# Eight weight tiles instead of six in the expert stages, and 2 KB runs for the context's weights

## The chip, the cores and the metric

One Trainium2 chip, one core. The metric is the device time of one execution in microseconds (us), the median of several runs. Tensors are float32 throughout. The core's engines are TensorE (PE; its weight loads are listed apart as PEld), VectorE (DVE), ScalarE (ACT), GpSimd (POOL) and SyncE (SP), and 16 DMA engines move data between device memory and the on-chip buffers. All weight loads here are issued by SP, in one queue and in the order of the program.

## What is computed

A network of two blocks over 256 tokens of 1024 features. The first block has two layers, each an attention or a retention followed by a mixture of 32 experts. The second block has two layers over the same tokens and over a separate context of 256 positions, each a mixer and a feed-forward of 2816 hidden units. The context needs its full first layer and part of its second, and does not depend on the tokens:

```python
# experts: each token goes to 2 of 32; every expert's weights are read
def expert_block(args):
    xb, e = args
    a, b = jnp.split(xb @ w_gu[e], 2, axis=-1)        # [1024, 2 * 512]
    return (jax.nn.silu(a) * b) @ w_down[e]           # [512, 1024]

# second block, for the tokens and for the context
def swiglu(h, w_gu, w_down):                          # [1024, 2 * 2816], [2816, 1024]
    gate, up = jnp.split(h @ w_gu, 2, axis=-1)
    return (jax.nn.silu(gate) * up) @ w_down

pc = (rmsnorm(xc, norm1_g[l]) * (1.0 + scc1) + shc1) @ w_in[l] + b_in[l]   # w_in [1024, 3088]
...
xc = xc + gc1 * (y_c @ w_out[l])
xc = xc + gc2 * swiglu(rmsnorm(xc, norm2_g[l]) * (1.0 + scc2) + shc2, w_gu[l], w_down[l])
```

## The kernel before

Features or tokens lie on 128 partitions. The program runs through stages: attention (from 0 us), the first expert stage (`moe(0)`), retention, the second expert stage (`moe(1)`), then the tokens' two layers of the second block. Beside each stage runs other work that does not depend on it: the context's mixer of layer 0 beside `moe(0)`, and the context's feed-forward of layer 0 and short mixer of layer 1 beside `moe(1)`. `weave` (L1737) traces the two together, R1 = 0.8 or R3 = 0.88 steps of the context's work for each step of the experts'. A scheduler then sets each engine's order from priorities; the engines run their lists in order.

Weights come as tiles of 1 MB ([128 partitions, 2048 numbers], 8 KB on each partition) from the pool `wp`, which has six of them (L97). `wt` (L126) hands them out. At the start of an expert stage three more places, `e0` to `e2` of another pool, are used once each. A load waits on SP until PE has read the tile that lay in its place before.

- `moe` (L848): the experts in eight groups of four, q = 0 to 7. A group loads 16 tiles for gate and up (L153, two experts' 128 rows of 1024 columns, runs of 4 KB) and 8 tiles for down. The products with gate and up are L956, with down L976. `gather` (L885) picks the next group's tokens. `combine` (L979) adds a group's result to the tokens: a copy `ys`, four products (L986) into PSUM banks `g`, four additions by DVE (L988).
- `fs` (L417): a product with features on partitions, for the context in plain float32 (mode "f"): blocks of 256 columns of all 1024 rows, one tile each, in runs of 1 KB. 16 products (L430; the trace lists each as two records) fill one bank `g`; then ACT or DVE reads it, and the step ends (`yield`).
- `ts` (L437): a product with tokens on partitions; blocks of 512 columns and 512 rows, runs of 2 KB.
- `ffn` (L1396): the feed-forward, in mode "f" in 11 rounds of 256 hidden units, three steps each: gate by `fs`, up by `fs`, and `down` (L1407) of the round before: four pairs of products (L1416), each into a bank `g` of its own, which `residual` (L369) multiplies (L372) and adds (L373) on DVE.
- `mixer` (L1263): the input products by `fs` and `ts`; the convolution's gate columns and its value columns are two calls of `fs` of 256 columns, which lie side by side in `w_in`.

There are four banks `g` (L100) for all of this, and two double banks `m` for the experts' sums.

Of the kernel before, what the change touches and what calls it, by code (L numbers as in the profile page):

```python
# [19 lines left out]
NEG = -1e30  # L20
RS = -8192.0                    # what rsqrt's scaled form carries
NE, CAP, FF = 32, 32, 512
R0, R1, R2, R3, R4 = 1.8, 0.8, 1.0, 0.88, 0.7           # steps of other work per step of the main path
AHEAD = 200                     # instructions that what the others wait for goes ahead of
TAPS = 6                        # convolution taps between other work
PIECE, WS = 512, 6              # elements per partition split at a time; pieces on chip
# [3 lines left out]
# columns of the constant array  # L30
C_ID, C_LE, C_LT, C_GE, C_ONE = 0, 128, 256, 384, 512
C_Z, C_LOW, C_UP = 640, 768, 896          # 0 where col <= row / col >= row, else NEG
C_IOTA, C_GRP, C_I8 = 1024, 1056, 1088
C_SEL, C_OFF = 1096, 1112                 # row 32 j + i, column i; rows of scales: what to add, 1 / RS
C_COS, C_SIN, C_RET = 1116, 1372, 1628         # rotary, decay
NCST = C_RET + 4 * 384

# modulation vectors: which third of the columns of w_mod, and which two of its quarters
# [4 lines left out]
def constants():  # L43
    """Tables that depend on shapes alone."""
# [35 lines left out]
class Tags:  # L80
    """A pool, some of whose tags lie in another one under other names."""
# [10 lines left out]
class Net:  # L92
    def __init__(self, tc, I, out, es):
# [8 lines left out]
        self.flip, self.extra = 0, []  # L102
        self.later, self.pending, self.taken = [], [], False
        self.early, self.hold = -99, None                  # pieces of weights whose low parts GpSimd makes

# [7 lines left out]
    def bank(self):  # L113
        """One bank, from the other pool while g's are taken."""
        return self.m()[:, 0:512] if self.taken else self.g()

    def two(self, mode, apart=False):
        """Two banks."""
        if mode == "f":
            return self.g(), self.g()  # L120
        if apart:
            return self.m()[:, 0:512], self.m()[:, 0:512]
        t = self.m()
        return t[:, 0:512], t[:, 512:1024]

    def wt(self, name):  # L126
        """A weight tile; some lie in the places of tiles that are no longer needed."""
        if self.extra:
            return self.pre.tile([P, 2048], F32, tag=self.extra.pop(0), name=name)
        return self.wp.tile([P, 2048], F32, tag="w", name=name)  # L130

    def wload(self, src):
        """One tile of weights: rows (k p) of src on the partitions."""
# [6 lines left out]
    def wtile(self):  # L140
        """A weight tile as [P, 2, D]."""
        return self.wt("w").rearrange("p (b d) -> p b d", b=2)

    def gain(self, src, g):
        """src [D] on all partitions."""
# [3 lines left out]
    def wload2(self, src):  # L149
        """The same rows of two experts: src [2, P, 1024]."""  # L150
# [16 lines left out]
    def affine(self, o, i, scale, bias=None, eng=None):  # L167
        """o = i * scale + bias, per partition."""
# [10 lines left out]
    def split(self, pool, tag, src, shape=None, low=None):  # L179
        """src = H + L exactly, both in the tensor engine's one-pass format."""  # L180
# [12 lines left out]
    def wparts(self, w, mode):  # L193
        """Parts of a weight tile [P, k, c]: each a function of (row block, first column, last column)."""
# [15 lines left out]
    def pairs(self, a, b):  # L210
        """Products that make up a.b for operands in parts."""
        return [(a[0], b[0])] if len(a) == 1 else [(a[0], b[0]), (a[1], b[0]), (a[0], b[1])]

    def rstd(self, ss, n, eps=EPS):
        """1/sqrt(ss/n + eps)"""
# [4 lines left out]
    def rsqrt(self, h, scaled=False):  # L220
        """1/sqrt(h): a first guess from the exponent's bits, then Newton's steps. Scaled: RS times it, for one column."""
# [9 lines left out]
        for _ in range(3):  # L231
            if scaled:                  # y = c / sqrt(h) to (y h y - 3 c c) y = -2 c^3 / sqrt(h)
# [13 lines left out]
    def rms(self, x, b, junk, act=False):  # L246
        """rstd of token block b of x [P, 2, D]"""
# [12 lines left out]
    def transposed(self, xn, b, cb):  # L260
        """cb(k, psum [P, n, 128]) for the feature chunks k .. k + n of token block b of xn [P, 2, D]"""
# [7 lines left out]
    def normed(self, pool, x, g, sh, mode, junk, tag="x", first=None, xn=None):  # L269
        """Parts of (rms-normalised x, times g plus sh)^T, each [P, 8, T]; sh and g / RS [P, D].  # L270
# [1567 lines left out]
```

## Time and profile before

| | |
|---|---|
| median of 3 runs | 2349.72 us (2346.77 to 2353.50) |
| span of the profiled execution, first to last instruction | 2346.0 us |
| PE busy | 2127.2 us, 91% of the span |
| DVE, ACT, POOL busy | 1060.9, 695.6, 172.9 us |
| moved by DMA | 686.64 MB, on average 293 GB/s |
| first expert stage, about | 208 to 762 us |
| second expert stage, about | 985 to 1635 us |

The profiled execution's own time is its span; what lies around the span in a timed run is not shown, and the median of the runs is 3.7 us above it. The page cuts the span into 40 slices of 58.65 us and gives for each the busy share of every engine, PE's granted clock and the mean busy share of the 16 DMA engines in tenths, and the GB/s moved. A table of stretches gives the same for any stretch, with idle time as length less busy time. A share of DMA of 1 or a little more in a stretch means that the DMA engines did not rest in it. A list of waits gives, for each line and tile, what it waited for: total, times, and the longest, in us.

### The profile page before, as it was taken

The numbers are of one execution on the slowest core, as the hardware profiler recorded it, in microseconds if no ns is written. First come the engines' busy times: TensorE is split into PE (matmuls) and PEld (weight loads), VectorE is DVE, ScalarE is ACT, GpSimd is POOL, SyncE is SP. The second block draws the span as 40 slices with busy tenths as digits, with TensorE's granted clock in tenths as the row PEclk, the third lists the DMA queues.
The fourth block names the chain that finished last, engine by engine and source line by source line (L and its number), as shares of the span: only waits on it lengthen the run. The fifth ranks groups of instructions, "written<-read, shape, count | busy, mean of one in ns | idle before, by whom it ended". The sixth has DMA issues, their size and how long they took to land. (4 is left out here: it accounts for less than half of the span.)

```text
span 2346.0 us, 32803 instructions
## 1 busy us (share of the span) xinstructions
PE 2127.2 (91%) x12844; PEld 1433.4 (61%) x12845; DVE 1060.9 (45%) x2513; ACT 695.6 (30%) x1420; POOL 172.9 (7%) x194
## 2 busy tenths in 40 slices
PE   8998899889877999989899999987998998998998
PEld 7765445344222776855444444334787997787997
DVE  6556053322101766531121221415778556777555
ACT  4353111211000434520000000012555554554554
POOL 1001000000000111010000000001212002102000
PEclk9999999999988999989999999999999999999999
DMA  8864999999999977579999999999756554555551
GB/s 257 313 245 166 350 399 392 369 399 378 379 409 384 323 281 246 203 268 382 391 398 393 399 390 390 367 356 346 256 162 202 188 190 156 187 181 171 192 185 63
DMA packets 305320, 686.64 MB, mean 293 GB/s; under 512 B 22056, under 2 KB 163784, under 8 KB 298888
## 3 DMA queue, kind: packets, MB, share of 16 engines
q1 hardware_dynamic: 305096, 684.45, 79.9%
q8 instruction: 103, 1.69, 0.3%
q14 instruction: 57, 0.47, 0.1%
q10 hardware_dynamic: 64, 0.03, 0.0%
HBM read 681.78 MB, written 2.62 MB: 292 GB/s over the span
## 5 line engine op out<-in xcount | busy, mean ns | idle before, releaser
L190 DVE TENSOR_TENSOR wl<-w,wh 128x512 fp32r<-128x512 f32 x574 | 396.3, 707 | 252.4 <-ACT wh L185 233.7
L185 ACT CAST wh<-w 128x512 fp32r<-128x512 f32 x600 | 364.3, 621 | 355.5 <-PE psm L430 111.6
L956 PE MATMUL psm<-w,xg 128*32 128x512 f32 x2048 | 319.8, 632 | 61.8 <-DMA w<-in_expert_w_gu_dram 55.0
L430 PE MATMUL psg<-xt,w 128*128 128x256 f32 x1056 | 235.8, 381 | 20.5 <-DMA w<-in_w_gu_dram 11.3
L430 PEld LDWEIGHTS psg<-xt,w 128*128 128x128 f32 x1056 | 198.0, 190 | 71.1 <-issue 38.6
L956 PEld LDWEIGHTS psm<-w,xg 128*32 128x32 f32 x2048 | 66.4, 112 | 270.6 <-issue 150.4
L430 PE MATMUL psg<-xh,wh 128*128 128x256 f32 x608 | 177.2, 291 | 3.9 <-ACT wh L185 2.4
L430 PE MATMUL psm<-xh,wh 128*128 128x256 f32 x640 | 179.9, 281 | 0.6 <-ACT ffh L1450 0.6
L430 PE MATMUL psm<-xh,wl 128*128 128x256 f32 x640 | 179.8, 281 | 0.0
L430 PE MATMUL psm<-xl,wh 128*128 128x256 f32 x640 | 179.7, 281 | 0.0
L430 PE MATMUL psg<-xh,wl 128*128 128x256 f32 x608 | 175.1, 288 | 2.4 <-DVE wl L190 2.4
L430 PE MATMUL psg<-xl,wh 128*128 128x256 f32 x608 | 173.8, 286 | 0.0
L976 PE MATMUL psm<-w,hT 128*32 128x512 f32 (+1 forms) x1152 | 156.7, 564 | 16.0 <-DMA w<-in_expert_w_down_dram 12.5
L430 PEld LDWEIGHTS psg<-xh,wh 128*128 128x128 f32 x608 | 118.1, 194 | 18.6 <-ACT wh L185 9.5
L430 PEld LDWEIGHTS psm<-xh,wh 128*128 128x128 f32 x640 | 120.7, 189 | 1.9 <-ACT ffh L1450 1.1
L430 PEld LDWEIGHTS psm<-xh,wl 128*128 128x128 f32 x640 | 120.6, 188 | 0.7
L430 PEld LDWEIGHTS psg<-xh,wl 128*128 128x128 f32 x608 | 118.0, 194 | 4.9 <-DVE wl L190 4.2
L430 PEld LDWEIGHTS psm<-xl,wh 128*128 128x128 f32 x640 | 120.8, 189 | 0.0
L430 PEld LDWEIGHTS psg<-xl,wh 128*128 128x128 f32 x608 | 117.9, 194 | 0.3 <-issue 0.2
L965 ACT ACTIVATE ha<-psm 128x512 f32<-128x512 f32 x16 | 9.6, 597 | 334.3 <-PE psm L956 334.3
L988 DVE TENSOR_TENSOR x<-x,psg 128x512 f32<-128x512 f32 (+1 forms) x72 | 45.1, 628 | 123.2 <-PE psg L986 123.0
L976 PEld LDWEIGHTS psm<-w,hT 128*32 128x32 f32 x1152 | 38.6, 111 | 93.2 <-issue 52.2
(497 smaller groups left out, 3263.9 us busy)
## 6 DMA issues: line engine op xcount, KB each, us to landing
w<-in_expert_w_gu_dram SPq DMA_DIRECT2D x256, 1024.0 KB
w<-in_expert_w_down_dram SPq DMA_DIRECT2D x112, 1024.0 KB
w<-in_w_gu_dram SPq DMA_DIRECT2D x66, 1024.0 KB
w<-in_w_mod_dram SPq DMA_DIRECT2D x48, 1024.0 KB
w<-in_w_in_dram SPq DMA_DIRECT2D x40, 1024.0 KB
w<-in_w_down_dram SPq DMA_DIRECT2D x33, 1024.0 KB
w<-in_ret_w_in_dram SPq DMA_DIRECT2D x24, 1024.0 KB
w<-in_fox_w_in_dram SPq DMA_DIRECT2D x16, 1024.0 KB
```

What stands on the lines that cost most here:

```text
L185: nc.scalar.copy(h, src)
L190: eng.tensor_tensor(l, src, h.bitcast(F32), op=ALU.subtract)
L430: self.nc.tensor.matmul(o, a, x, start=i == 0, stop=i == len(mm) - 1)
L956: nc.tensor.matmul(gu[32 * j:32 * j + 32, half * 512:(half + 1) * 512], xg[:, k, 32 * j:32 * j + 32], ws[j // 2][:, j % 2, half * 512:(hal ...
L965: nc.scalar.activation(ha, gu[:, 0:512], AF.Silu)
L976: nc.tensor.matmul(o[32 * j:32 * j + 32, :], hT[:, k, 32 * j:32 * j + 32], w(j), start=k == 0, stop=k == 3)
L988: v.tensor_tensor(o, o, ps, op=ALU.add)
```

## The change

The change does three things. In the expert stages `wt` hands out tiles in turn from `ring`: six of `wp` and two of a new pool `more`, which exists only inside `moe`; to make room, `combine`'s copy `ys` shares the places of `ha`, and in the second expert stage the context's tile `kt` takes the place of the tokens' `hs`. Second, in mode "f" a product of `fs` with a multiple of 512 columns goes to `fs_wide`: blocks of 512 columns, loaded as two tiles of 512 rows in runs of 2 KB, with a step after each; two banks `g` are held from the first tile to the second. The convolution's two calls become one of 512 columns. Third, the context's feed-forward is `ffn_wide`: five rounds of 512 units and one of 256, with `down_wide` in steps of 256 rows as before. The number of products, of bytes and of steps stays the same. The remaining lines of the diff take out comments.

```diff
+        self.ring, self.turn = [self.wp] * 6, 0
...
     def wt(self, name):
         if self.extra:
             return self.pre.tile([P, 2048], F32, tag=self.extra.pop(0), name=name)
-        return self.wp.tile([P, 2048], F32, tag="w", name=name)
+        self.turn = (self.turn + 1) % len(self.ring)
+        return self.ring[self.turn].tile([P, 2048], F32, tag="w", name=name)
...
     def fs(self, xin, wsrc, cb, mode, between=None, middle=None):
         n = wsrc.shape[1]
+        if mode == "f" and n % 512 == 0:
+            yield from self.fs_wide(xin[0], wsrc, cb)
+            return
...
+    def fs_wide(self, x, wsrc, cb):
+        for n0 in range(0, wsrc.shape[1], 512):
+            ps = self.g(), self.g()
+            for k0 in (0, 4):
+                w = self.wload(wsrc[k0 * P:(k0 + 4) * P, n0:n0 + 512])
+                for c in range(4):
+                    o = ps[c // 2][:, c % 2 * T:c % 2 * T + T]
+                    for k in range(4):
+                        self.nc.tensor.matmul(o, w[:, k, c * P:(c + 1) * P], x[:, k0 + k, :],
+                                              start=k0 == 0 and k == 0 and c % 2 == 0, stop=k0 == 4 and k == 3 and c % 2 == 1)
+                if k0 == 0:
+                    yield
+            for c in range(4):
+                cb(n0 // P + c, ps[c // 2][:, c % 2 * T:c % 2 * T + T])
+            yield
...
     def moe(self, l):
...
+            self.ring = [self.wp] * 6 + [pool("more", 2)] * 2
...
-                    ys = m2.tile([P, n], F32, tag="ys", name="ys")
+                    ys = m2.tile([P, n], F32, tag="ha", name="ys")
...
+            self.ring = [self.wp] * 6
...
     def ffn(self, l, i, mode, bp, b2):
...
+        if mode == "f":
+            yield from self.ffn_wide(l, i, xin[0], bp, b2)
+            return
...
+    def ffn_wide(self, l, i, x, bp, b2):
+        nc, I, v = self.nc, self.I, self.nc.vector
+        w_gu, w_dn = I["w_gu_2"][l], I["w_down_2"][l]
+        t = self.x if i == 0 else self.ctx
+        todo = None
+        for c0 in range(0, FFN, 512):
+            n = min(512, FFN - c0)
+            h = b2.tile([P, 4, T], F32, tag="w0", name="ffh")[:, :n // P]
+            yield from self.fs((x,), w_gu[:, c0:c0 + n], lambda j, ps: nc.scalar.activation(h[:, j, :], ps, AF.Silu), "f")
+            yield from self.fs((x,), w_gu[:, FFN + c0:FFN + c0 + n],
+                               lambda j, ps: v.tensor_tensor(h[:, j, :], h[:, j, :], ps, op=ALU.mult), "f")
+            if c0 == 0:
+                g2 = self.row(l, "g2", i, bp.tile([P, D], F32, tag="kt", name="g2"), "f")
+            if todo:
+                yield from self.down_wide(t, w_dn, g2, *todo)
+            todo = (c0, h)
+        yield from self.down_wide(t, w_dn, g2, *todo)
+
+    def down_wide(self, x, w_dn, g, c0, h):
+        nc = self.nc
+        for k0 in range(0, h.shape[1], 2):
+            w = self.wload(w_dn[c0 + k0 * P:c0 + (k0 + 2) * P, :])
+            for half in range(2):
+                for b in range(2):
+                    o = self.g()
+                    for k in range(2):
+                        nc.tensor.matmul(o, h[:, k0 + k, b * P:(b + 1) * P], w[:, k, half * 512:(half + 1) * 512],
+                                         start=k == 0, stop=k == 1)
+                    self.residual(x[:, b, half * 512:(half + 1) * 512], o, g[:, half * 512:(half + 1) * 512], b, False)
+            yield
...
-            yield from self.fs(xin, w_in[:, CONV_OFF + 256:CONV_OFF + 512], lambda j, ps: nc.scalar.activation(
-                ag[:, j, :], ps, AF.Sigmoid, bias=L["bg"][:, j:j + 1]), mode)
-            next(six)
+            cgate = lambda j, ps: nc.scalar.activation(ag[:, j, :], ps, AF.Sigmoid, bias=L["bg"][:, j:j + 1])
+            if mode == "r":
+                yield from self.fs(xin, w_in[:, CONV_OFF + 256:CONV_OFF + 512], cgate, mode)
+                next(six)
...
+                yield from self.fs(xin, w_in[:, CONV_OFF:CONV_OFF + 512], conv, mode)
+                next(six)
...
-            bp = Tags(bp, self.pre, {"rows": "e0", "xn": "e1", "xt": "e2"})
+            bp = Tags(Tags(bp, self.pre, {"rows": "e0", "xn": "e1", "xt": "e2"}), self.px, {"kt": "hs"})
```

What the scheduler makes of it, on SP at the start of the second expert stage. `w<-in_expert_w_gu` is a tile of the experts, `w<-in_w_gu` one of the context's feed-forward, `rb` and `rows` are small vectors, and the `TENSOR_LOAD` reads the experts' counts, which DVE writes after the router. Before:

```order
L153 DMA w<-in_expert_w_gu_dram 128x2x1024 x7
L571 DMA rb<-in_b_in_dram 128x512
L572 DMA rb<-in_b_in_dram 128x256
L573 DMA rb<-in_sgu_ln_g_dram 128x256
L574 DMA rb<-in_sgu_ln_b_dram 128x256
L576 DMA rb<-in_sgu_b_dram 64x128 x3
L137 DMA w<-in_w_gu_dram 128x8x256
L576 DMA rb<-in_sgu_b_dram 64x128
L1236 DMA rows<-modd_1055 128x2x512 x2
L1024 TENSOR_LOAD cnti
L1024 ISA x2
L153 DMA w<-in_expert_w_gu_dram 128x2x1024 x4
```

The same place in the changed kernel:

```order
L155 DMA w<-in_expert_w_gu_dram 128x2x1024 x7
L139 DMA w<-in_w_gu_dram 128x4x512
L155 DMA w<-in_expert_w_gu_dram 128x2x1024
L593 DMA rb<-in_b_in_dram 128x512
L594 DMA rb<-in_b_in_dram 128x256
L595 DMA rb<-in_sgu_ln_g_dram 128x256
L596 DMA rb<-in_sgu_ln_b_dram 128x256
L598 DMA rb<-in_sgu_b_dram 64x128 x3
L155 DMA w<-in_expert_w_gu_dram 128x2x1024
L598 DMA rb<-in_sgu_b_dram 64x128
L1260 DMA rows<-modd_1055 128x2x512 x2
L1048 TENSOR_LOAD cnti
```

Ten weight tiles instead of eight are ahead of the `TENSOR_LOAD`; two of the experts' loads moved there from behind it.

On PE in the middle of the second expert stage, one stretch of a context round between the experts' products. `psg<-xt,w` is `fs`, `psg<-w,ffh` is `down`, `psg<-ys,sgt` is `combine`. Before:

```order
L1416 MATMUL psg<-w,ffh 128x512 x8
L956 MATMUL psm<-w,xg 32x512 x16
L430 MATMUL psg<-xt,w 128x256 x16
L956 MATMUL psm<-w,xg 32x512 x8
L986 MATMUL psg<-ys,sgt 128x512
L956 MATMUL psm<-w,xg 32x512 x2
L986 MATMUL psg<-ys,sgt 128x512 x3
L956 MATMUL psm<-w,xg 32x512 x6
L430 MATMUL psg<-xt,w 128x256 x16
```

In the changed kernel:

```order
L1539 MATMUL psg<-w,ffh 128x512 x8
L999 MATMUL psm<-w,hT 32x512 x16
L1539 MATMUL psg<-w,ffh 128x512 x8
L979 MATMUL psm<-w,xg 32x512 x16
L451 MATMUL psg<-xt,w 128x256 x16
L979 MATMUL psm<-w,xg 32x512 x8
L1009 MATMUL psg<-ys,sgt 128x512
L979 MATMUL psm<-w,xg 32x512 x2
L1009 MATMUL psg<-ys,sgt 128x512 x3
L979 MATMUL psm<-w,xg 32x512 x6
L451 MATMUL psg<-xt,w 128x256 x16
```

Two steps of down now follow each other with 16 expert products between them, and the two L451 rows here are the first and second half of one block, with a `combine` between them. Of the 15 blocks of `fs_wide`, 4 have a `combine` between their halves, 7 have transposes or a part of `gather`, and 4 have the experts' products alone.

## Rows read from the trace of the kernel before

**Rows 1.** The page's 40 slices: DMA share, GB/s.

```profile
DMA  8864999999999977579999999999756554555551
GB/s 257 313 245 166 350 399 392 369 399 378 379 409 384 323 281 246 203 268 382 391 398 393 399 390 390 367 356 346 256 162 202 188 190 156 187 181 171 192 185 63
```

**Rows 2.** Stretches, first expert stage: from:to, length, each engine's busy us, clock, DMA, GB/s.

```profile
208.00:221.00 13.00, 11.39 (x78) 6.91 (x78) 7.26 (x32) 2.79 (x12) 1.47 (x4) 0.77 0.12 32
221.00:254.00 33.00, 31.66 (x146) 13.15 (x146) 10.50 (x13) 4.36 (x7) 5.38 (x5) 1.00 0.86 323
254.00:386.00 132.00, 118.80 (x708) 66.11 (x703) 44.81 (x133) 18.40 (x37) 1.71 (x5) 0.99 1.03 398
386.00:443.00 57.00, 52.54 (x366) 27.39 (x359) 30.80 (x108) 18.93 (x61) 3.12 (x4) 1.00 0.91 353
443.00:574.00 131.00, 110.95 (x609) 53.36 (x602) 21.21 (x64) 18.70 (x31) 5.92 (x10) 0.97 1.03 400
574.00:614.00 40.00, 35.89 (x161) 11.99 (x159) 8.30 (x12) 0.00 (x0) 0.00 (x0) 1.00 0.90 337
614.00:762.00 148.00, 109.32 (x598) 33.23 (x599) 14.71 (x28) 8.76 (x19) 0.16 (x2) 0.87 1.03 399
```

**Rows 3.** The same table, second expert stage; engines in order PE, PEld, DVE, ACT, POOL.

```profile
985.00:1018.00 33.00, 26.39 (x153) 18.62 (x151) 17.33 (x90) 10.81 (x27) 1.58 (x5) 0.79 0.40 103
1018.00:1080.00 62.00, 60.64 (x356) 38.34 (x352) 12.08 (x22) 8.82 (x18) 6.14 (x7) 1.00 0.92 346
1080.00:1386.00 306.00, 283.90 (x1478) 149.90 (x1475) 66.83 (x112) 17.46 (x42) 3.03 (x8) 1.00 1.03 396
1386.00:1436.00 50.00, 47.49 (x235) 23.24 (x234) 12.58 (x20) 1.24 (x3) 0.00 (x0) 1.00 0.99 377
1436.00:1500.00 64.00, 57.93 (x297) 27.62 (x296) 15.71 (x26) 3.90 (x9) 0.00 (x0) 1.00 1.03 404
1500.00:1545.00 45.00, 41.22 (x178) 17.24 (x178) 19.60 (x37) 6.36 (x15) 4.47 (x4) 0.96 0.80 304
```

**Rows 4.** The same table: saturated stretches of 1 KB, 2 KB and 4 KB runs.

```profile
1140.00:1142.00 2.00, 2.00 (x18) 0.55 (x11) 0.00 (x0) 0.00 (x0) 0.00 (x0) 1.00 1.10 353
1153.50:1156.50 3.00, 3.00 (x27) 0.96 (x29) 0.00 (x0) 0.66 (x2) 0.00 (x0) 1.00 1.09 345
936.00:941.00 5.00, 5.00 (x24) 4.12 (x23) 4.79 (x20) 1.52 (x3) 0.00 (x0) 1.00 1.04 387
1164.00:1176.00 12.00, 10.71 (x49) 3.93 (x48) 3.53 (x6) 0.00 (x0) 0.00 (x0) 1.00 1.03 413
```

**Rows 5.** Waits of SP's DMA queue, 1018 to 1545 us: total, times, longest.

```profile
SPq L153 <- PE psg L430: 155.7, 22, 8.9
SPq L153 <- PE psm L956: 107.8, 55, 9.4
```

**Rows 6.** Waits of PE, 1080 to 1500 us.

```profile
PE psm L956 <- DMA w<-in_expert_w_gu_dram: 11.8, 15, 1.6
PE psg L430 <- DMA w<-in_w_gu_dram: 11.3, 12, 1.2
PE psg L1416 <- DMA w<-in_w_down_dram: 3.7, 5, 0.8
```

**Rows 7.** Waits of PE, 1545 to 1613 us.

```profile
PE psm L956 <- PEq L1027: 5.0, 1, 5.0
PE psg L430 <- DMA w<-in_w_in_dram: 1.2, 1, 1.2
```

**Rows 8.** Timeline of PE near 1110 us: start, length, line, count.

```profile
1109.65 7.17 PE L430 MATMUL psg<-xt,w 128*128 128x256 f32 x32
1130.80 7.10 PE L1416 MATMUL psg<-w,ffh 128*128 128x512 f32 x16 [0.75 <-DMA w<-in_w_down_dram]
```

**Rows 9.** Groups of DVE, 1018 to 1545 us: busy, mean ns, idle before, releaser.

```profile
L372 DVE TENSOR_TENSOR psg<-psg,g 128x512 f32<-128x512 f32 x44 | 30.8, 700 | 45.2 <-PE psg L1416 45.2
L988 DVE TENSOR_TENSOR x<-x,psg 128x512 f32<-128x512 f32 x24 | 16.5, 688 | 55.4 <-PE psg L986 55.4
```

More of the change, by code (lines that the diff above doesn't have):

```diff
@@ L1297, in mixer, with conv @@
             yield
-            yield from self.fs(xin, w_in[:, CONV_OFF:CONV_OFF + 256], glu, mode)
+            if mode == "r":
+                yield from self.fs(xin, w_in[:, CONV_OFF:CONV_OFF + 256], glu, mode)
+            else:
+                held = {}
+                def conv(j, ps):
+                    held[j] = ps
+                    if j == 3:
+                        for k in range(2):
+                            cgate(k, held[2 + k])
+                        for k in range(2):
+                            glu(k, held[k])
+                yield from self.fs(xin, w_in[:, CONV_OFF:CONV_OFF + 512], conv, mode)
+                next(six)
             gates = self.gates(bp, next(six))
@@ L1466, in ffn @@
         yield
+    def ffn_wide(self, l, i, x, bp, b2):
[22 more added lines that the diff above has]
+                    o = self.g()
+                    for k in range(2):
+                        nc.tensor.matmul(o, h[:, k0 + k, b * P:(b + 1) * P], w[:, k, half * 512:(half + 1) * 512],
+                                         start=k == 0, stop=k == 1)
+                    self.residual(x[:, b, half * 512:(half + 1) * 512], o, g[:, half * 512:(half + 1) * 512], b, False)
+            yield
     def gates(self, bp, gc):
```

## The prediction

> **What bounds the kernel now.** I read the page's slices first. Of the 40, the two expert stages fill about 20, and there alone the DMA engines are busy at 9 tenths in nearly every slice, at 370 to 400 GB/s; in the other stages they rest a third or half of the time [rows 1]. So the change, which touches little outside the expert stages, is to be judged there. Next came the table of stretches, with borders where the GB/s change. The reader is to see two kinds of stretch in turn. In the long ones, 254 to 386, 443 to 574 and 614 to 762 us, DMA moves 398 to 400 GB/s without rest, while PE idles for 132 - 118.8 = 13.2, 20.1 and 38.7 us: the transfers set the pace [rows 2]. In the short ones between them DMA moves 323, 353 or 337 GB/s, and PE idles less: PE sets the pace, all six tiles hold weights that it has not read, and SP waits. The second stage has the same pattern, with PE nearer to full: 60.6 of 62 us at its start, 22.1 us idle from 1080 to 1386, 6.1 from 1436 to 1500 [rows 3]. The lists of waits confirm both: SP waits 156 us for context products L430 to free a tile and 108 for expert products L956 [rows 5], and PE's idle time from 1080 to 1500 is mostly for landing weights, 11.8 + 11.3 + 3.7 us in the three largest rows [rows 6]. One context step is 7.1 us of PE for one tile [rows 8], during which DMA can fill nearly three; the experts' products free tiles faster than DMA fills them. The six tiles are there to even this out.
>
> **Part 1: longer runs.** The prices are in three saturated stretches. With runs of 1 KB the rate is 353 and 345 GB/s, with 2 KB 387, with 4 KB 413 [rows 4]. A tile of 1.0486 MB thus takes 3.01 us (at 348), 2.71 and 2.54 us, and a tile that goes from 1 KB to 2 KB saves 0.30 us of DMA. The change moves 30 tiles: 20 of the feed-forward's 22 gate and up tiles (2816 is five blocks of 512 and one of 256, which stays as it is) and 2 of the short mixer's keys in the second stage; 2 each of convolution, keys, queries and output gate in the first, 8. The most is 30 x 0.30 = 9.0 us. It counts only where PE later waits for DMA. In the first stage all 8 tiles have such a stretch behind them. In the second about five tiles are loaded before 1080, where PE is full, and two near the end; I take 15. That is 23 x 0.30 = **6.9 us**; the ends are 0 and 9.0.
>
> What the row shows here is that a shorter run costs rate: 1 KB against 4 KB loses 16% [rows 4]. The Trainium skill ("DMA: Bandwidth & Descriptors", Specifications) puts the least transfer for line rate at 512 B. By that rule this part would bring nothing and the sum below would be smaller by these 6.9 us; the three rates of this trace disagree with it.
>
> **Part 2: two more tiles.** They let DMA run two tiles further ahead: 2 x 2.54 = 5.1 us of transfers. In a stretch where PE sets the pace and DMA rests, DMA does that much more before it fills up, and in the next DMA-bound stretch PE waits that much less. So each such stretch gives the smallest of three: what DMA loses in it, 5.1 us, and what PE afterwards waits for DMA. Losses against 400 GB/s: 221 to 254 us, 33 x (1 - 323/400) = 6.4, and nearly all of the 13 us before, where the router blocks SP [rows 2]; 386 to 443, 6.7; 574 to 614, 6.3; 1018 to 1080, 8.4, and 24.5 in the 33 us before; 1386 to 1436, 2.9; 1500 to 1545, 10.8 [rows 3]. The three stretches of the first stage are followed by 13.2, 20.1 and 38.7 us of idle PE, so each gives 5.1. The start of the second gives 5.1 as well: its two tiles are the ones that the order now puts ahead of the wait for the counts. There DMA gets ahead while PE is full until 1080, so the gain appears only after that. From 1386 to 1436 I take 2 of 2.9, since some of that loss is the slower runs. The stretch from 1500 is the doubtful one: behind it PE waits for DMA only 1.2 us, and 5.0 us at a branch that no tile shortens [rows 7], so I take 1.2. Sum 4 x 5.1 + 2 + 1.2 = **23.6 us**. The ends are 0, if every stretch that is filled only moves its wait, and 5 x 5.1 + 2.9 = 28.4. In the second stage the total up to 1500 is 5.1 + 2 + 15 x 0.30 = 11.6 us, out of 22.1 + 6.1 = 28.2 us of PE idle in the two long stretches: it fits, though both engines are then within a few per cent of full.
>
> **Part 3: banks held.** `fs_wide` holds two of the four banks `g` from its first half to its second, while the experts go on between. Nothing in this trace holds them so beside a `combine`, so I bound it. Below: no cost, because DVE today waits for PE at these places, 55.4 us before L988 and 45.2 us before L372, not the reverse [rows 9]. A gain is excluded: a held bank lets nothing start earlier. Above: in 11 of 15 blocks something that needs banks stands between the halves, and each waits for four additions of 0.69 us, 2.75 us, 30 us in all. I take one addition in each of the 4 blocks with a `combine`, **2.8 us** lost, near the lower end because of that row.
>
> **Nothing else.** Products, bytes, steps and their weave are equal in number. Down steps now come in pairs, 2 x 7.1 us of PE with 16 expert products between; eight tiles are 20 us of DMA, so they cover it, where six would be 15. The up products' reader is now four operations of DVE at the end of two tiles instead of two after each; the next step of PE works on other banks and hides it, and without that cover it would be two operations more, at most 2 x 0.70 us per block by L372's price [rows 9]. `ys` in the place of `ha` waits for transposes that are done a group earlier. The retention's and the tokens' stages have the same SP lists as before.
>
> **The sum.** 6.9 + 23.6 - 2.8 = 27.7 us. From the profiled span, 2346.0 - 27.7 = 2318.3; the median of the runs is 3.7 above the span, so 2322 us.
>
> **Rivals.**
> (a) *Only the first stage gives.* PE is so full in the second that what DMA saves there turns into waits of PE for banks, DVE or its branch. Then 3 x 5.1 + 8 x 0.30 - 1 = 16.7, 2333 us. For it: 60.6 of 62 us and 47.5 of 50 busy [rows 3]; against it: the 26.8 us of [rows 6].
> (b) *More than two tiles' worth.* Where PE-bound and DMA-bound pieces change within microseconds, as from 574 to 614 and inside 1080 to 1500, a deeper buffer removes several small waits in one stretch. If half of PE's idle time of 28.2 us in the second stage's long stretches and of 72 us in the first's goes [rows 2, 3], 50 us, less the 2.8 of the banks: 2346 - 47.3 + 3.7, about 2302 us.
> (c) *The change does nothing measurable.* The six tiles already cover what can be covered, the added depth shifts each wait to the next one, and the runs give 5 us: 2345 us. For it: DMA reads 396 to 404 GB/s in every long stretch, and no buffer makes a full queue faster. Against it: those stretches follow losses that add up to over 40 us, outside the two router gaps.
> (d) *Slower: banks.* If every `fs_wide` waited both at its start for the two multiplications and additions of a down step before it (2 x 1.39 us) and between its halves for a `combine` (2.75), that is 5.5 us in each of 15 blocks, 83 us; it decides from 30.5 / 15 = 2.0 us per block on. At 3.0 us it gives 45 - 30.5 = 14.5 us lost, 2364 us. Against it: 16 expert products stand ahead of each block, and DVE's waits in [rows 9].
>
> **How the numbers follow.** A measurement of this kernel can tell about 0.3%, 7 us, from no change. The forecast itself, 2310 to 2329, gets 0.47; (a), (b), (c) and (d) get 0.17, 0.13, 0.13 and 0.10. Faster by over 7 us are the forecast, (a) and (b): 0.77; within 7 us (c): 0.13; slower (d): 0.10. The range reaches from (b), 2302, to just short of no change, 2346, and holds the forecast, (a), most of (b) and part of (c); (d) and the rest stay outside.
>
> **What would show it.** In the profile after, the stretches that now read 323, 353 and 337 GB/s in the first stage should be shorter or near 400; the first stage should end some 17 us earlier against its start, the second 12 us. Saturated stretches with feed-forward weights should read 385 or so instead of 350. PE's waits for weights from 1080 to 1500 should fall from 28 to about 16 us. L986's counterpart should show a few waits for DVE, under 3 us. I am wrong if PE's waits for weights stay while DMA shows no rest, or if idle time before the half blocks names DVE or ACT.

## The result, and the profile after

The changed kernel takes 2310.75 us (median of 4 runs, 2308.65 to 2313.84) against 2348.24 for the kernel before, measured beside it: a ratio of 0.984, 95% interval 0.9825 to 0.9852, or 37.5 us less. The forecast was 27.7 us less, 2322 us; the range, 2302 to 2346, holds the result. The profiled execution has a span of 2311.9 us, 34.1 less than that of before.

Where the time went, by four events of PE that both traces have (the routers' first product, L868 before and L891 after; the retention's first transposes; the context's norm of layer 1; the tokens' norm at the end of the second expert stage). Single executions, so a difference of 2 us says little here: the tokens' layers, whose code is the same, take 705 to 709 us in the profiles of this study. The forecast's -11.6 holds no cost of the banks; with the 1.8 us of it that the prediction leaves for the second stage it is -9.8.

| us | before | after | difference | forecast |
|---|---|---|---|---|
| start to router 1 | 208.9 | 209.8 | +0.9 | 0 |
| router 1 to retention (first expert stage) | 561.4 | 544.1 | -17.3 | -17 |
| retention to router 2 | 234.1 | 234.2 | +0.1 | 0 |
| router 2 to the context's norm | 510.5 | 494.7 | -15.8 | -11.6, or -9.8 with the banks |
| the context's norm to the tokens' norm | 125.0 | 120.4 | -4.6 | about -1 |
| tokens' layers | 706.1 | 708.7 | +2.6 | 0 |

The last two events of the changed kernel are these groups of L268 (duration min/median/max, first and last start):

```profile
L268 PE MATMUL psg<-cst,xn x16: 272/273/328, 1482.8 to 1486.2; 128*128 128x128 f32 x16
L268 PE MATMUL psg<-cst,w x16: 421/421/476, 1603.2 to 1606.5; 128*128 128x128 f32 x16
```

The page's slices after, DMA share in tenths and GB/s, to be laid beside [rows 1]. In the expert stages the slices that were under 400 GB/s between others at 400 have nearly gone, and the six full slices of the second stage read 402 to 408 where they read 390 to 399. The third line is the page's count of packets: 15,360 fewer than before (305,320), which is 30 tiles of 1,024 runs that became 512 each.

```profile
DMA  8865999999999877679999999999755554655551
GB/s 259 313 242 180 364 402 407 374 402 402 408 406 381 317 273 261 226 272 386 407 406 405 408 406 402 386 387 296 253 160 191 183 186 143 208 180 168 183 183 64
DMA packets 289960, 686.64 MB, mean 297 GB/s; under 512 B 22056, under 2 KB 133064, under 8 KB 283528
```

Stretches of the first expert stage after (columns as in [rows 2]). The stretch from 574 to 614, which moved 337 GB/s with the DMA engines at 0.90, moves 405 without rest; of the dip of 57 us at 353 GB/s, 18 us at 295 are left; the one from 222 is as it was, 328.

```profile
222.00:254.00 32.00, 30.68 (x146) 12.72 (x142) 10.49 (x13) 4.36 (x7) 5.38 (x5) 1.00 0.87 328
254.00:425.00 171.00, 159.07 (x1002) 89.09 (x994) 66.22 (x205) 32.63 (x77) 3.66 (x8) 0.99 1.03 404
425.00:443.00 18.00, 16.42 (x106) 6.63 (x104) 9.67 (x36) 4.74 (x19) 1.18 (x1) 0.91 0.76 295
443.00:574.00 131.00, 116.00 (x628) 55.52 (x624) 25.45 (x70) 14.96 (x28) 5.94 (x10) 0.96 1.03 404
574.00:614.00 40.00, 35.08 (x168) 14.02 (x167) 5.26 (x8) 2.47 (x3) 0.00 (x0) 0.96 1.03 405
614.00:747.00 133.00, 90.52 (x552) 27.32 (x550) 13.61 (x26) 8.03 (x19) 0.16 (x2) 0.99 1.03 397
```

The second stage after, the stretches of [rows 3] moved by the 16 us that its router now comes earlier. From 1064 to 1370 PE is busy for 291.37 of 306 us, 95%, where it was 283.90, 93%; the stretch after it has gone from 377 to 404 GB/s, the last from 304 to 361.

```profile
1002.00:1064.00 62.00, 60.18 (x355) 38.23 (x354) 12.37 (x23) 9.52 (x19) 6.14 (x7) 1.00 0.93 354
1064.00:1370.00 306.00, 291.37 (x1554) 159.06 (x1553) 62.75 (x107) 18.23 (x44) 3.03 (x8) 0.99 1.03 404
1370.00:1420.00 50.00, 47.61 (x243) 21.52 (x245) 16.05 (x25) 2.21 (x5) 0.00 (x0) 1.00 1.03 404
1484.00:1529.00 45.00, 38.49 (x210) 16.96 (x211) 14.29 (x29) 6.78 (x13) 4.43 (x3) 1.00 0.94 361
```

PE's waits from 1064 to 1484 (total, times, longest), which answer to [rows 6]. For weights they are 5.8 + 4.4 + 1.8 + 0.7 + 0.4 = 13.1 us, where [rows 6] had 26.8 (29.2 with a fourth row of 2.4 us) and about 16 were forecast. The largest row is now PE's wait for `ha`, the experts' hidden units, which DVE multiplies and PE then transposes (L992); before it was 1.4 us in this stretch. It is no wait for a weight tile, and it comes back below. None names a bank, or DVE's additions that would free one.

```profile
PE psg L992 <- DVE ha L989: 5.9, 4, 1.5
PE psm L979 <- DMA w<-in_expert_w_gu_dram: 5.8, 8, 1.5
PE psg L1539 <- DMA w<-in_w_down_dram: 4.4, 6, 0.7
PE psg L451 <- DMA w<-in_w_gu_dram: 1.8, 2, 0.9
PE psm L999 <- DMA w<-in_expert_w_down_dram: 0.7, 2, 0.4
...
PE psg L435 <- DMA w<-in_w_gu_dram: 0.4, 1, 0.4
```

### The profile page after: what moved, and what is told of

Its sections match the earlier page's. It is cut to its first block, busy times and chain, and to the rows that moved or that the text cites. A ratio compares the mean times of both kernels' runs of the same rounds, so it can differ in the third digit from the quotient of the medians.

```text
span 2311.9 us, 32779 instructions
## 1 busy us (share of the span) xinstructions
PE 2109.6 (91%) x12844; PEld 1434.3 (62%) x12845; DVE 1063.3 (46%) x2513; ACT 693.6 (30%) x1418; POOL 173.1 (7%) x194
## 5 line engine op out<-in xcount | busy, mean ns | idle before, releaser
L979 PE MATMUL psm<-w,xg 128*32 128x512 f32 x2048 | 300.3, 612 | 49.1 <-DMA w<-in_expert_w_gu_dram 44.5
L451 PE MATMUL psg<-xt,w 128*128 128x256 f32 x960 | 214.0, 381 | 4.3 <-DMA w<-in_w_in_dram 2.5
L979 PEld LDWEIGHTS psm<-w,xg 128*32 128x32 f32 x2048 | 65.1, 111 | 240.2 <-issue 145.7
L451 PEld LDWEIGHTS psg<-xt,w 128*128 128x128 f32 x960 | 180.1, 190 | 44.5 <-issue 16.2
L999 PE MATMUL psm<-w,hT 128*32 128x512 f32 (+1 forms) x1152 | 154.6, 567 | 15.6 <-DMA w<-in_expert_w_down_dram 9.7
L435 PEld LDWEIGHTS psg<-xh,wh 128*128 128x128 f32 x608 | 118.6, 195 | 18.5 <-ACT wh L187 9.4
L989 DVE TENSOR_TENSOR ha<-ha,psm 128x512 f32<-128x512 f32 x16 | 11.0, 686 | 245.8 <-ACT ha L988 245.8
```

Source lines behind the costliest of these rows:

```text
L435: self.nc.tensor.matmul(o, a, x, start=i == 0, stop=i == len(mm) - 1)
L451: self.nc.tensor.matmul(o, w[:, k, c * P:(c + 1) * P], x[:, k0 + k, :], start=k0 == 0 and k == 0 and c % 2 == 0, stop=k0 == 4 and k == 3 a ...
L979: nc.tensor.matmul(gu[32 * j:32 * j + 32, half * 512:(half + 1) * 512], xg[:, k, 32 * j:32 * j + 32], ws[j // 2][:, j % 2, half * 512:(hal ...
L999: nc.tensor.matmul(o[32 * j:32 * j + 32, :], hT[:, k, 32 * j:32 * j + 32], w(j), start=k == 0, stop=k == 3)
```

## The experiments

All medians, with the ratio to the kernel before measured in the same series; the interval of each ratio is about 0.0015 to either side, 3 to 4 us. The diffs are against the changed kernel. The last three columns are lengths from the profiles, as in the table above.

| kernel | tiles | context's blocks | median us | ratio | first stage | router 2 to context's norm | from there to tokens' norm |
|---|---|---|---|---|---|---|---|
| before | 6 | 256, 1 KB | 2348.2 to 2351.3 | 1 | 561.4 | 510.5 | 125.0 |
| ring_only | 8 | 256, 1 KB | 2315.76 | 0.9853 | 545.8 | 498.3 | 124.7 |
| ring_other | 8 | 256, 1 KB | 2315.88 | 0.9855 | 545.3 | 498.5 | 121.3 |
| ring_long | 8 | 256, 2 KB | 2306.73 | 0.9815 | 541.5 | 492.7 | 120.1 |
| wide_only | 6 | 512, 2 KB | 2349.31 | 0.9992 | 565.2 | 511.4 | 123.7 |
| first_only | 8, then 6 | 512, 2 KB | 2331.59 | 0.9921 | 544.7 | 511.0 | 123.3 |
| ring7 | 7 | 512, 2 KB | 2323.97 | 0.9886 | 551.2 | 498.0 | 119.1 |
| after | 8 | 512, 2 KB | 2310.75 | 0.9839 | 544.1 | 494.7 | 120.4 |
| wide_1k | 8 | 512, 1 KB, two transfers | 2311.06 | 0.9829 | 542.5 | 498.5 | 119.8 |
| wide_2x | 8 | 512, 2 KB, two transfers | 2303.44 | 0.9805 | 542.6 | 493.2 | 116.2 |
| no_yield | 8 | 512, half the steps | 2342.78 | 0.9970 | 558.9 | 399.8 | 234.5 |
| no_hold | 8 | 512, tiles in a row | 2317.53 | 0.9862 | 547.2 | 496.9 | 121.0 |
| ring8s | 8, single copies | 512, 2 KB | 2309.94 | 0.9827 | 544.6 | 494.9 | 118.6 |
| ring9s | 9, single copies | 512, 2 KB | 2295.74 | 0.9769 | 538.3 | 489.9 | 120.4 |

### Each part alone: ring_only and wide_only

```diff
 ring_only
-        if mode == "f" and n % 512 == 0:
+        if False:
             yield from self.fs_wide(xin[0], wsrc, cb)
 (the same for ffn_wide and the convolution's two calls)

 wide_only
-            self.ring = [self.wp] * 6 + [pool("more", 2)] * 2
```

> Two more weight tiles in both expert stages, the context's blocks left at 256 columns with 1 KB runs and its feed-forward at 256 units, as in the kernel before. Theory 1 (the prediction's sizes: depth 23.6, the rest of the gain from elsewhere): 2348.2 - 23.6 = 2324.6 us, first stage 15 us shorter than before, second about 8. Theory 2 (depth also takes the small waits in the steady part of the second stage, so that all that was missing in the sum is depth's): 2348.2 - 33 = 2315 us, second stage 16 to 18 us shorter. Theory 3 (the wide blocks are worth more than their longer runs, depth less): over 2330 us.

> Blocks of 512 columns with 2 KB runs and feed-forward steps of 512 units, with six weight tiles all through, as in the kernel before. Theory 1: longer runs +6.9, two banks held -2.8: 2348.2 - 4.1 = 2344.1 us, with the second stage 3 to 5 us shorter and the first about the same. Theory 2 (all that was missing is depth's): the same, 2344 us. Theory 3 (wide blocks worth more): 2348.2 - 14 = 2334 us or less. If holding two banks costs anything with six tiles, over 2346 us.

Measured: 2315.76 and 2349.31 us. The depth alone brings 34.6 us where the whole change brings 37.5; the wide blocks alone bring 1.1 us, nothing that can be told from zero. That is theory 2, and by 11 us more than the prediction gave to depth. wide_only missed its 2344 us by 5, and lies where its last sentence expected a cost of the banks, but PE's waits in its trace name no bank either, which speaks for another reason (below).

In the first stage the places that the prediction named show it. Stretches of before, counted from its router (columns as in [rows 2]; the first lies around the router):

```profile
178.90:221.90 43.00, 36.39 (x213) 27.15 (x215) 24.59 (x101) 16.43 (x39) 2.08 (x6) 0.88 0.33 107
385.90:442.90 57.00, 52.54 (x366) 27.49 (x362) 30.90 (x108) 19.03 (x61) 3.12 (x4) 1.00 0.91 352
573.90:613.90 40.00, 35.99 (x161) 12.09 (x159) 8.30 (x12) 0.00 (x0) 0.00 (x0) 1.00 0.90 337
```

and the same of ring_only, 1.5 us later throughout:

```profile
180.40:223.40 43.00, 35.32 (x200) 26.05 (x199) 23.91 (x100) 15.36 (x38) 2.08 (x6) 0.84 0.47 147
387.40:444.40 57.00, 52.62 (x355) 26.17 (x354) 26.76 (x90) 17.50 (x55) 3.12 (x4) 0.97 0.96 378
575.40:615.40 40.00, 35.08 (x164) 12.86 (x160) 5.54 (x9) 2.46 (x3) 0.00 (x0) 0.96 1.03 406
```

More moved in each: 43 us x 40 GB/s = 1.72 MB, 57 x 26 = 1.48, 40 x 69 = 2.76. Two tiles are 2.1 MB. The first two places give less than that. The third gives more than two tiles' worth because it is not one place: in slices of half a microsecond before's loads nearly stop twice in it, near 578 and near 607 us, at the price of about 1.0 and 1.3 MB, and in ring_only neither stop is left. At 400 GB/s the three are 14.9 us, and the stage is 15.6 us shorter.

In the second stage the steady part shows what was missed. These are the 377 us that begin 103 us after the router, in before, in wide_only, in ring_only and in ring_long (which follows below):

```profile
1107.40:1484.40 377.00, 348.34 (x1840) 183.55 (x1839) 78.87 (x135) 21.36 (x51) 3.03 (x8) 1.00 1.03 394
```

```profile
1109.80:1486.80 377.00, 347.27 (x1812) 178.95 (x1809) 83.77 (x141) 20.79 (x49) 3.02 (x8) 1.00 1.01 394
```

```profile
1093.30:1470.30 377.00, 353.62 (x1853) 184.43 (x1851) 85.40 (x144) 21.34 (x51) 3.02 (x8) 1.00 1.03 401
```

```profile
1088.80:1465.80 377.00, 359.18 (x1875) 187.11 (x1874) 87.54 (x147) 21.44 (x52) 3.03 (x8) 1.00 1.03 406
```

Six tiles move 394 GB/s there, whatever the runs; eight move 401 with 1 KB runs and 406 with 2 KB. The 7 GB/s between six and eight tiles are dips of a microsecond or two that a stretch of 300 us averages away. Here are two of them in before, in the DMA share and GB/s of 40 slices of half a microsecond from 1384.4 us:

```profile
DMA  9999999659699999699999999999999999999999
GB/s 410 401 434 401 393 401 418 262 197 319 279 418 418 418 377 279 221 336 352 385 385 385 393 418 385 401 426 426 418 418 389 365 395 348 352 354 361 387 383 416
```

and the same 20 us, counted from the router, in ring_only:

```profile
DMA  9999999999999999999999999999999999999999
GB/s 426 393 401 410 385 397 408 389 373 371 385 365 377 375 385 371 379 399 393 410 418 410 426 393 401 418 393 418 418 410 426 389 385 403 377 389 377 360 375 369
```

What stands before the first dip is in PE's timeline of before (start, length, line, count): products L895 that gather the next experts' tokens and read no weights, drawn between the down products, and behind them a context step L430 of 7.07 us that frees its tile only at its end, 1387.5. The last two rows are SP's: it issues no load between 1379.5 and 1387.58, so all that was free had been filled by then.

```profile
1375.76 1.50 PE L895 MATMUL psg<-oh,xn 128*128 128x128 f32 x12
1377.19 1.91 PE L976 MATMUL psm<-w,hT 128*32 128x512 f32 x12
1379.04 1.60 PE L895 MATMUL psg<-oh,xn 128*128 128x128 f32 x12
1380.48 7.07 PE L430 MATMUL psg<-xt,w 128*128 128x256 f32 x32
1379.14 0.37 SPq L137 DMA_DIRECT2D w<-in_w_down_dram  x1
1387.58 3.94 SPq L153 DMA_DIRECT2D w<-in_expert_w_gu_dram  x4
```

Half-microsecond slices under 340 GB/s in those 377 us: 37 in before, 48 in wide_only, none in ring_only. Without them the mean is 400 GB/s in before and 405 in wide_only, the rates of eight tiles; they lose 5.6 us against 401 GB/s in before, and 10.4 against 406 in wide_only. So in this part, with six tiles, the dips ate what the longer runs gave.

Why wide_only has more of them is argued and not shown. Quicker loads may only come to the next full point sooner. But the wide form also has another order on PE, which makes it wait longer for `ha`, and a PE that stands still frees no tile. From 210 to 1640 us these waits are, in before, ring_long, wide_only, the changed kernel and wide_2x (below):

```profile
PE psg L969 <- DVE ha L966: 11.3, 8, 1.5
PE psg L1000 <- DVE ha L997: 12.8, 8, 2.8
PE psg L991 <- DVE ha L988: 19.0, 12, 3.0
PE psg L992 <- DVE ha L989: 18.8, 12, 2.8
PE psg L995 <- DVE ha L992: 14.4, 9, 2.8
```

The longer runs alone with six tiles, which would tell, were not run.

### The runs' length: ring_long and ring_other, wide_1k and wide_2x

```diff
 ring_long, in fs of ring_only
-            w = self.wparts(self.wload(wsrc[:, n0:n0 + nn]), mode)
+                self.loading = self.nc.sync.dma_start(long.rearrange("p (k c) -> p k c", c=512),
+                    self.I["w_gu_2"][0][h0:h0 + 512, m0:m0 + 512].rearrange("(k p) c -> p k c", p=P))
+                w = self.wparts(long.rearrange("p (k c) -> p k c", c=256), mode)
 ring_other
+                w = self.wparts(self.wload(self.I["w_gu_2"][0][:, c0:c0 + 256]), mode)

 wide_1k, in fs_wide
-                w = self.wload(wsrc[k0 * P:(k0 + 4) * P, n0:n0 + 512])
+                for c0 in (0, 256):
+                    self.nc.sync.dma_start(w[:, :, c0:c0 + 256],
+                        wsrc[k0 * P:(k0 + 4) * P, n0 + c0:n0 + c0 + 256].rearrange("(k p) c -> p k c", p=P))
 wide_2x
+                for j in (0, 2):
+                    self.nc.sync.dma_start(w[:, j:j + 2, :],
+                        wsrc[(k0 + j) * P:(k0 + j + 2) * P, n0:n0 + 512].rearrange("(k p) c -> p k c", p=P))
```

> ring_only, with the 1 KB runs of the context's 256-column blocks made 2 KB runs: each block's tile is loaded with as many bytes of other weights, in rows of 512 columns, so that only the length of the runs differs and the context comes out wrong. Theory 1 (23 tiles that the load of a saturated stretch waits for, by 0.30 us): 6.9 us under ring_only. By the ends of that term: 0 to 9.0 us under it. If the wide form's structure, not its runs, were worth something: within 2 us of ring_only.

> ring_long with runs of 1 KB: each of the context's narrow tiles is loaded from the same other weights as there, by 256 columns, so the context comes out wrong too; against ring_long (2306.7) only the runs differ, against ring_only (2315.8) only the place of the data. If the 9 us between those two are the runs' length: 2316 us. If they are the place: 2307 us.

> The changed kernel, with each wide tile loaded by two transfers of 256 columns, 1 KB runs; all else as in the changed kernel. Theory 1: 2310.7 + 6.9 = 2317.6 us (ends 2310.7 and 2319.7). If the runs' length costs nothing here: 2310.7 us. If what the wide form gains is its structure: within 2 us of the changed kernel.

> The changed kernel with each wide tile loaded by two transfers of 256 rows and 2 KB runs, against wide_1k with two transfers of 256 columns and 1 KB runs (2311.1): the same number of transfers of the same size, only the runs differ. If the runs' length is worth its rate (mean rates of the second stage's steady part 405 against 401, some 4 to 7 us in both stages): 2304 to 2307 us. If length is worth nothing in the total: 2311 us. If the changed kernel's single transfers are the better ones: over 2313 us.

Measured: 2306.73 against 2315.88 with the same other weights in 1 KB runs, 9.2 us for 33 tiles, 0.28 each; ring_other equals ring_only, so the place of the data is nothing. Both pairs are clean: their orders on PE and on SP are the same throughout. In the wide form 2303.44 against 2311.06, 7.6 us for 30 tiles, 0.25 each (5.6 by the ratios, since these two ran in different series). The 0.30 that [rows 4] gave holds, and with eight tiles it is worth most of its price on nearly every tile. The Trainium skill ("DMA: Bandwidth & Descriptors", Specifications) puts the least transfer for line rate at 512 B; the two pairs disagree with that, as [rows 4] did.

wide_1k missed its expectation: it was to be 6.9 us over the changed kernel and is level with it. The pair explains it only half: wide_2x, with the changed kernel's runs, is 7.3 us better than it (2303.44 against 2310.75), which hid the shorter runs in wide_1k. That this is what two transfers for a tile are worth is not shown, because the edit does more than the diff says: the scheduler gave the kernels with two transfers another order. On PE the transposes of `ha` went behind the context's step at several places, for example here, the first two rows of the changed kernel, the last two of wide_2x:

```profile
1110.10 0.66 PE L992 MATMUL psg<-cst,ha 128*128 128x128 f32 x4 [1.48 <-DVE ha L989]
1110.81 7.07 PE L451 MATMUL psg<-xt,w 128*128 128x256 f32 x32
1104.49 7.17 PE L454 MATMUL psg<-xt,w 128*128 128x256 f32 x32
1111.50 0.60 PE L995 MATMUL psg<-cst,ha 128*128 128x128 f32 x4
```

The wait is gone there, and 4.4 us of such waits in the second stage (the rows above). Of the 7.2 us by which the profiles differ, 1.5 us are in each of the first two columns and 4.2 in the last; 3.1 of these are PE's busy time for the same products, 95.09 us at a mean granted clock of 0.97 against 98.22 at 0.94. How the 7.3 us divide among the transfers, the order and the clock is open.

### Where the depth pays, and how far: first_only, ring7, ring8s, ring9s

```diff
 first_only
-            self.ring = [self.wp] * 6 + [pool("more", 2)] * 2
+            if not l:
+                self.ring = [self.wp] * 6 + [pool("more", 2)] * 2
 ring7
+            self.ring = [self.wp] * 6 + [pool("more", 1)] * 1
 ring8s, and ring9s with 3 instead of 2
-                xg = m2.tile([P, 8, P], F32, tag="xg", name="xg")
+                xg = mp.tile([P, 8, P], F32, tag="xg", name="xg")
 (the same for hT and og; the overflow's hidden units go to a weight tile, gov to the place of rk)
```

> The changed kernel with the two tiles in the first expert stage alone; the second has six. By the stages of the profiles (first stage 17.3 shorter, second 20.4): 2348.2 - 17.3 = 2331 us. Rival (a) of the prediction put it at 2333. If the second stage's gain were the wide blocks' and not the tiles': 2315 us or less.

> The changed kernel with one more weight tile in the expert stages where it has two. If each tile is worth the same (the prediction's rule: 2.54 us of loading at each place where the loads run dry; two tiles measured 34.6): 2311 + 17 = 2328 us. If the first tile takes most of it (the waits are short, and the second covers the rest of them alone): 2322 us or less. If only the second brings the loads over a whole expert-free piece (a threshold): 2334 us or more.

> The changed kernel with three more tiles instead of two; room for the third comes from single copies of the gathered tokens, the transposed hidden units and the placed gates, which had two each. If each tile is worth 17 us: 2294 us. If the loads are near full rate already (399 to 406 GB/s over the stages' steady part, 413 for 4 KB runs): 2311 - 3 = 2308 us. If the single copies make the experts wait: over 2313 us.

> ring9s without the ninth tile: eight tiles, single copies of the gathered tokens, the hidden units and the placed gates. If ring9s' 15 us are the tile's: 2311 us, and more if the single copies cost something. If they come from the single copies: 2296 us.

Measured: with the tiles in the first stage alone 2331.59, rival (a)'s price (2333). From wide_only that is 17.7 us for the first stage, and 20.8 for the second from there to the changed kernel. The second stage gives, and at least about as much as the first (by the ratios 16.7 and 19.3, a difference within the intervals).

By number of tiles, all in the wide form: 2349.31, 2323.97, 2310.75, 2295.74 for 6, 7, 8 and 9. The steps are 25.3, 13.2 and 15.0 us (the ninth against ring8s 14.2; by the ratios 24.9, 11.0 and 16.4). ring7 lies between the two it was expected at, 2328 if all tiles are worth the same and 2322 or less if the first takes most. The seventh closes most of the dips of the steady part (from 48 slices under 340 GB/s in wide_only to 4, at 405 GB/s): router 2 to the context's norm falls by 13.4 us with it, and by 3.3 with the eighth. The eighth and ninth are worth 11 to 16 us each, and no end of that is reached here. ring8s, level with the changed kernel, shows that the single copies cost nothing and that the ninth tile's gain is the tile's. The expectation that the loads were near full rate already was wrong: the steady part reads 406 GB/s with eight and with nine tiles, so what a tile still buys lies outside it. Against ring8s it is 6.3 us in the first stage (544.6 to 538.3) and 5.0 from router 2 to the context's norm (494.9 to 489.9); there ring9s moves 253 GB/s in the 43 us before the router, where ring8s moves 231, and 338 in the 103 us behind it against 329, together 1.9 MB or 4.6 us at 406 GB/s. At 425 to 443 us ring9s moves 376 GB/s where the changed kernel moved 295:

```profile
425.00:443.00 18.00, 13.93 (x106) 5.21 (x104) 7.08 (x30) 3.56 (x14) 0.00 (x0) 1.00 0.95 376
```

ring9s, 2295.74 us, ratio 0.977 (0.9755 to 0.9783), is the fastest kernel of the study. With two transfers for each wide tile it might be faster still; that was not run.

### The banks, and the steps: no_yield and no_hold

```diff
 no_yield, in fs_wide
-                if k0 == 0:
-                    yield
 no_hold: the same, and behind the block
             yield
+            yield
```

> The changed kernel without the step between the two tiles of a wide block: both tiles' products stand in a row, so that no bank is held over an expert's work. If holding costs what the prediction took (2.8 us): 2308 us. If nothing: 2311 us. If two tiles' products in a row (14.3 us) make the loads run dry again behind eight tiles: 2316 us or more, the second stage longer by it.

> no_yield with an empty second step behind each wide block, so that the context advances at the same pace against the experts as in the changed kernel; only the two tiles' products stand in a row, and no bank is held over an expert's work. If no_yield's 32 us were the pace (the context done early and the experts left alone for the loads): within 3 us of the changed kernel, 2311, or 2308 if the held banks cost 2.8. If they were the 14.3 us of products in a row, which eight tiles don't cover: 2335 us or more.

Measured: 2342.78 and 2317.53. Without the step between the halves nearly the whole gain is gone, though there are eight tiles; no_yield's expectation had only the banks and the products in a row, and took 2316 us for the sign of the latter. The two stretches of no_yield's second stage, from its router to the context's norm and from there to the tokens' norm:

```profile
1001.90:1401.70 399.80, 391.89 (x2040) 228.47 (x2040) 115.38 (x214) 31.01 (x77) 14.14 (x20) 0.99 0.94 363
1401.70:1636.20 234.50, 178.91 (x1079) 77.69 (x1079) 54.35 (x167) 27.63 (x57) 14.56 (x14) 0.96 1.00 384
```

The context takes half the steps, is drawn in at the same number of steps for each of the experts', and is done 95 us earlier (399.8 against 494.7). In the first 400 us PE is nearly full, 392 us busy, and DMA rests at times, 363 GB/s. The context's last products end at 1482 us, and the experts are alone from there; in the 234.5 us PE idles for 55.6, 24.9 of them for this one row:

```profile
PE psm L977 <- DMA w<-in_expert_w_gu_dram: 24.9, 23, 1.5
```

no_hold, with the pace put back, recovers 25.3 of the 32.0 us. So most was the pace of the context against the experts. Its time lies between its two expectations: the other 6.8 us (5.4 by the ratios) are what two tiles' products in a row cost, with the order on PE that comes of them, less what a held bank may cost; both stages are 3 us longer than the changed kernel's. Not holding the banks is no faster, and no wait names them; a cost of under some 4 us can't be excluded by this, since the two came together.

## Why the prediction was right, and where its sizes were off

**What bounds the kernel.** Right. The gain lies in the expert stages and nowhere else, in the stretches between full and empty tiles.

**Part 1, longer runs, 6.9 us.** Right in size at eight tiles: 7.6 and 9.2 in the two pairs, near the upper end, 9.0, since nearly every tile counts. The two parts were added as if independent; but at six tiles the wide form with its longer runs is worth 1.1 us in all. Whether the runs need the depth, or the form's order ate them there, is open.

**Part 2, depth, 23.6 us.** The mechanism was right, the term too small: ring_only measures 34.6. In the first stage 15.3 was forecast and 15.6 found, though not place by place: 574 to 614 was counted as one place of at most two tiles, but it holds two stops of the loads and gave 6.9 us (2.76 MB), and the place at 386 gave 3.7 instead of 5.1. The stretch 222 to 254 itself did not rise; its gain came with the loads ahead of the router, as the sum had it. In the second stage 8.3 was forecast; the profiles of ring_only and ring_other, which run the same work, are 12.5 and 15.7 us shorter. The step that failed is the reading of [rows 3]: 396 GB/s from 1080 to 1386 was taken for a full queue. It was dips to 200 or 300 GB/s of a microsecond or two, 5.6 us in all, in a rate that is 400 without them. This is rival (b)'s mechanism, at a part of its price, and PE's 11.8 + 11.3 us in [rows 6], which the sum used only as a ceiling, were its trace. These 4 to 7 us are not all of the 11 that the term was short of: ring_only's profiled execution was itself 4.9 us above the median of its runs, so the rest can't be put to a place. The 3.2 us between the two are mostly the last piece, where PE is busy 100.41 us at a clock of 0.92 in ring_only and 97.23 at 0.95 in ring_other.

**Part 3, banks, -2.8 us.** Not borne out: PE's waits show no bank, where "a few waits for DVE" were forecast, and no_hold doesn't gain. Still the changed kernel is 4.0 us slower than ring_long, which has the same tiles and three more long ones (0.9 us); some 3 us of the wide form with one transfer remain. wide_2x, which holds the same banks, doesn't have them. What the traces show in this place is the wait for `ha`, 18.8 us against 12.8 in ring_long; how much of it ends up in the total is not shown. The sum had no term for it: the paragraph "Nothing else" counted products, bytes and steps, which are indeed equal, and put a changed order at nothing.

**The end of the second stage, 1.2 us.** 4.6 came. The wait of 1.2 us for a tile that the term stands for is gone. [rows 7]'s branch wait of 5.0 us appears after as 1.8 us of issue and 1.3 for DVE's sequencer at L979 and 1.6 for ACT's at L1009, 0.3 less in all. Most of the rest is the clock: PE's busy time for the same products is 2.5 us less, at a mean granted clock of 0.94 where it was 0.92 (before, then after):

```profile
1514.90:1639.90 125.00, 100.70 (x634) 52.61 (x634) 43.88 (x145) 21.70 (x44) 13.81 (x12) 0.92 0.95 347
1482.80:1603.20 120.40, 98.22 (x635) 52.59 (x635) 44.63 (x145) 21.58 (x44) 13.84 (x12) 0.94 0.97 356
```

The piece takes 116 to 125 us in the study's profiles, no_yield aside.

**From span to median, 3.7 us.** In every later run an execution's own time is 1.7 to 2.1 us above its span, so this step alone put the forecast about 2 us too high.

**The rivals.** (a) fell: first_only costs what it said, but the second stage gives 20.8 us more. (c) fell for the whole change; wide_only, the blocks without the tiles, is what looks like it. (d) fell with part 3. (b) holds in kind for the steady part of the second stage.

## What to carry to other kernels

A mean rate near the full one over hundreds of microseconds can still hide a per cent or two in dips shorter than a load; look at half-microsecond slices before calling a queue full, and take the rate of a slice without dips as what is to be had. Where DMA-bound and PE-bound pieces alternate, another tile of buffer can be worth up to its load time at each place where the loads stop (two tiles moved 1.5 to 2.8 MB more at the three places looked at here, one of which holds two stops). Gains from longer runs and from depth are not to be added unless each was measured beside the other. An edit of the loads alone can change the order of another engine: compare the orders of two kernels before a difference is put down to the edit. Merging two small steps of interleaved work into a larger one changes its pace against the other work as well, and in this kernel that cost nearly four times what the products in a row cost.

## What the runs showed that was not expected

The ninth tile still brings 14.2 us, as much as the eighth, with the loads of the steady part already at 406 GB/s. The kernel with two transfers of 512 KB in place of one of 1 MB for each wide tile is 7.3 us faster, with another order on PE and 4.4 us less of its waits for `ha`; what the transfers themselves are worth is not shown.
